# Exact products in three passes of 256 columns, or in one of 512 and one of 256

## The chip, the cores and the metric

One Trainium2 chip, one core. The metric is the device time of one execution of the whole program in microseconds (us); the median of the runs counts, and less is better.

## What is computed

A transformer of two different blocks on 256 tokens of width 1024, in fp32 throughout. Block 1 is an FFN (SwiGLU), a mixer (pooling and dilated attention, with gates) and a second FFN, each ahead of a residual sum with modulated norms. Block 2 is two layers of a mixer (retention, windowed attention, latent attention) and a mixture of 16 experts.

```python
def swiglu(u, w_in, w_out):
    a, b = jnp.split(u @ w_in, 2, axis=-1)
    return (jax.nn.silu(a) * b) @ w_out
...
        u = modulate(rmsnorm(h, g_norm_ffn1[l]), sh1, sc1)
        h = h + 0.5 * gt1 * swiglu(u, w_ffn1_in[l], w_ffn1_out[l])
        u = modulate(rmsnorm(h, g_norm_mix[l]), sh2, sc2)
        h = h + gt2 * token_mixing(u, cos, sin, w_in[l], w_pool[l], pool_scale[l],
                                   w_pool_branch[l], w_attn_branch[l], w_out[l])
```

The output is compared with an fp32 result, so that the large products have to keep nearly all the bits of fp32.

## The kernel before

**Layout.** Activations are held transposed: a tile of 128 features by 256 tokens is a block, and a tensor of width 1024 is eight blocks. Weights come from HBM in panels of 1 MB (1024 rows by 256 columns) into `raw` tiles, of which there are five (`raw_tile`, line 208).

**Exact products.** An fp32 number is split into a high part, rounded to the type fp32r, and the low rest (`split`, line 253): a cast on ScalarE and a subtraction on VectorE, both recorded at line 254. Weights are split half a panel at a time into `hl` tiles, of which there are six (`weights`, line 214); the raw tile is free when both halves are split. A product of a 128 by 128 block of weights with a block of activations is then three passes of TensorE into the same 256 columns of PSUM, low times low being left out:

```python
        def mm3(o, wh, wl, xh, xl, first, last):
            PE.matmul(o, wh, xh, start=first, stop=False)
            PE.matmul(o, wh, xl, start=False, stop=False)
            PE.matmul(o, wl, xh, start=False, stop=last)
```

These are lines 249 to 251. Where the tokens are the rows of the output, the activations are the stationary operand and the weights stream past: `proj_n` (lines 674 to 676) and `natural` (lines 1025 to 1027). Each pass loads its own stationary operand.

**PSUM** has eight banks of 512 fp32 columns. `mmtile` takes one of two banks in turn as two halves of 256 columns; the other six serve norms, attention and the like. Nothing reads a bank while passes into it are open, so the two halves of a bank are finished together.

**Stages.** The *first FFN* (`ffn`, line 552) begins with three pairs of panels as the modulation comes in (`begin`); from pair 3 on, a pair `a`, `b` of panels gives two feature blocks, one after the other, with `a` and `b` in the halves of one bank. ScalarE applies Silu to the first half (line 589), VectorE multiplies the second by it (line 590), and the product is split into the tiles gh and gl. Its output half runs over eight feature blocks: 22 block products into the first half of a bank, then one VectorE step that adds the gated sum to the residual hT (line 604), then the operand of the next step (`lead.add`) and its square for the norm. The *second FFN* does the same for pairs 1 to 10, after an opening pair.

The *first mixer* (`mixer`, line 704) computes queries and keys (two blocks of a panel in the halves of a bank, then `rotate`), values and the pool branch (`proj_n`, two token blocks in a bank), then for four heads the scores, the two gates (line 813, Tanh over the whole bank at line 815) and the values, then merges the branches and runs the output projection (line 837, VectorE step at line 838). In the FFNs and the mixer further columns of the modulation are computed on the side by VectorE from 1 MB tiles of w_ada (`ada`, line 354), some steps at a time where the code says `drain`; they use raw tiles too.

The *mixers of block 2* (`mixer2`, line 1014) use `natural` and `transposed` in the same way. Their output projection takes a panel at a time with its two feature blocks in one bank, the blocks of the inner dimension in the order 2, 3, 4, 5, 0, 1, 6, 7 (the attention outputs that are ready first come first), for panels 0 to 2, and one bank for each feature block in panel 3; VectorE adds the sums to hT (line 1319), and TensorE transposes finished blocks (line 1284) for the router. The *experts* (lines 1502 on) don't use these products.

**Order of the work.** The program is written in dataflow order; a planner puts each engine's instructions in a fixed order by its own estimate of when each becomes ready, earlier ones in the text first, and adds the semaphores. On the chip each engine works through its list and waits where an operand isn't ready. All weights are fetched from the queue of SyncE (SP).

Of the kernel before, what the change touches and what calls it, by code (L numbers as in the profile page):

```python
# [37 lines left out]
    # rotate-half permutation for two stacked heads of 64  # L38
# [9 lines left out]
    # partial sums: rows 0 and 32 of one kind, 64 and 96 of another  # L48
# [26 lines left out]
    # trailing mean minus token, transposed: [token in, token out]  # L75
# [9 lines left out]
    # retention decay with the 1/sqrt(dk) of the keys, [key, query]  # L85
# [9 lines left out]
    # router helpers: iota - 512 over slots; the lead by which f comes before e in a group of four  # L95
# [23 lines left out]
def layout(inputs):  # L119
    """Only moves data: every array keeps its type and values."""  # L120
# [27 lines left out]
    pair = [0, 3, 1, 4, 2, 5]      # heads whose keys lie in the first / second half, in turn  # L148
# [24 lines left out]
# ---------------------------------------------------------------- kernel  # L173
def body(tc, A, out, dbg=None, stop=None):
# [3 lines left out]
    with ctx:  # L178
# [22 lines left out]
        # ------------------------------------------------------------ streams  # L201
# [12 lines left out]
        class weights:  # L214
            """fp32 weights [128, kb, n] from DRAM, split exactly into hi + lo, in two halves, of which
            some are made at once and the others when first used."""

            def __init__(self, ap, kb, n, by="c", made=2):
# [6 lines left out]
                self.parts = [None, None]  # L225
# [4 lines left out]
            def make(self, i):  # L230
                if self.parts[i] is None:
# [5 lines left out]
                    self.parts[i] = (h, l)  # L237
                return self.parts[i]

            def at(self, k, a=None, b=None):  # L240
                """hi and lo of block k, columns a to b (all by default)."""
# [5 lines left out]
        def mm3(o, wh, wl, xh, xl, first, last):  # L247
            """o += w^T x, both operands split; only lo*lo (below fp32) is left to rounding."""
# [3 lines left out]

        def split(hi, lo, x):
            return S.copy(hi, x), V.tensor_tensor(out=lo, in0=x, in1=hi.bitcast(F32), op=ALU.subtract)  # L254

        def xtile(tag, dt=F32R, name=None):
            """[128, KB, T + 2], or that much of another use."""
            return xp.tile([P, KB * (T + 2)], dt, name=name or tag, tag=tag)

        class Lead:  # L260
            """A tensor's split product with its gains, made block by block as its sums become known: the first
            products of the next step run on it, and what is the same for all features of a token is applied to them.
            Further columns, an even number, hold vectors that are added to each token, so that their products come along.
            The normalised tensor takes its place."""

            def __init__(self, scale, extra=()):
                h, l = (xtile(t).rearrange("p (k t) -> p k t", k=KB) for t in ("xh", "xl"))
                self.h, self.l = h[:, :, :T], l[:, :, :T]
# [12 lines left out]
            def products(self, ws, banks, ks):  # L281
                """Of the four blocks of columns of two panels, a bank each."""
# [10 lines left out]
        # ------------------------------------------------------------ start  # L293
# [72 lines left out]
        def busy(n, tag="w"):  # L366
            """Keeps the clock of the tensor engine up over a wait: products that nothing reads."""
# [36 lines left out]
        class Norm:  # L404
            """Mean square over features of a transposed [128, KB, T] tensor, block by block."""
# [26 lines left out]
        def rows_to(rb, r):  # L432
            """Per-token columns [128, 2] as a row over all partitions: PSUM [128, T]."""
# [7 lines left out]
        def row(rb):  # L441
            """A row from PSUM in SBUF."""
# [4 lines left out]
        def lead_in(nrm, i, lead, ws, banks):  # L447
            """The first products, and the normalised tensor in place of their operand: rmsnorm(h) * scale + shift."""
# [9 lines left out]
        def norm_mod(rb, h, i, hi, lo):  # L458
            """hi + lo = rmsnorm(h) * scale + shift."""
# [7 lines left out]
        def first_rstd():  # L467
            """1 / rms of the input, as a row."""
# [83 lines left out]
        def ffn(f, nrm, i, side, n_in, n_out, lead, then, pq, start=None):  # L552
            with tc.tile_pool(name=f, bufs=1, reuse_waits="tile") as pool:
# [11 lines left out]
                for j in range(NJ):  # L565
# [1256 lines left out]
```

## Time and profile before

| | |
|---|---|
| time, median of 3 runs | 1182.7 us (1182.67 to 1187.75) |
| profiled execution, span (its own time is shown as the span alone) | 1186.2 us |
| TensorE (PE) busy | 1144.6 us, 96%, 8495 passes |
| weight loads (PEld) busy | 943.5 us, 80% |
| VectorE (DVE) busy | 713.3 us, 60% |
| ScalarE (ACT) busy | 511.4 us, 43% |
| GpSimd (POOL) busy | 44.5 us, 4% |
| mean granted TensorE clock | 0.987 of 2.4 GHz |
| HBM | 269.63 MB read, 228 GB/s over the span |

The profile is one execution, taken by the hardware profiler. A pass of TensorE is shown from its start to the modelled end of its result, and passes overlap: their mean length (some 280 ns) is not what each costs in a row of many; that is the distance from start to start, called pitch here. An engine's idle time is put down to the instruction that ended it.

### The profile page before, as it was taken

Reading aid. Unit: us, or ns where it says so; the run is one execution under the profiler, and the core shown is the slowest. Engines: PE = TensorE matmul, PEld = TensorE weight load, DVE = VectorE, ACT = ScalarE, POOL = GpSimd, SP = SyncE. Lnnn points to the kernel's source line nnn. Section 1 sums busy time; section 2 is a strip of 40 time slices with the busy share of each in tenths; the row PEclk is TensorE's granted clock in tenths of the full one; section 3 lists DMA queues with packets and bytes.
Section 4 is the critical chain, followed back from the end, with each engine's and each line's share of the span. In section 5 each row is a group of like instructions: output and inputs, shape, how many; then the busy total and the mean of one; then the engine's idle time right before and its main releaser. Section 6 shows DMA issues by size and latency. Waiting matters only on the chain. (4 is left out here: it accounts for less than half of the span.)

```text
span 1186.2 us, 20785 instructions
## 1 busy us (share of the span) xinstructions
PE 1144.6 (96%) x8495; PEld 943.5 (80%) x8495; DVE 713.3 (60%) x1410; ACT 511.4 (43%) x946; POOL 44.5 (4%) x53
## 2 busy tenths in 40 slices
PE   6999999999999999999999998999989999899995
PEld 4999999988888999999997878544458787844443
DVE  5698879777877775555677754621258864451114
ACT  4454445534534554444556434222247643322213
POOL 0000001000000200000120001000001000100000
PEclk9999999999999999999999999999989999999998
DMA  9788779738863455535572439599743334779941
GB/s 317 292 362 307 288 258 325 263 133 316 306 230 112 173 180 182 184 125 183 168 250 99 143 109 353 216 385 390 290 155 135 136 109 170 288 272 397 380 156 38
DMA packets 77354, 272.12 MB, mean 229 GB/s; under 512 B 7873, under 2 KB 10817, under 8 KB 62914
## 3 DMA queue, kind: packets, MB, share of 16 engines
q1 hardware_dynamic: 77250, 270.70, 62.8%
q8 instruction: 70, 1.15, 0.4%
q14 instruction: 34, 0.28, 0.1%
HBM read 269.63 MB, written 1.05 MB: 228 GB/s over the span
## 5 line engine op out<-in xcount | busy, mean ns | idle before, releaser
L254 DVE TENSOR_TENSOR hl<-raw,hl 128x1024 fp32r<-128x1024 f32 (+5 forms) x267 | 293.4, 1108 | 120.8 <-ACT hl L254 120.0
L254 ACT CAST hl<-raw 128x1024 fp32r<-128x1024 f32 (+5 forms) x267 | 254.0, 958 | 233.9 <-PE mm L251 172.2
L249 PE MATMUL mm<-xh,hl 128*128 128x256 f32 x896 | 255.2, 286 | 4.0 <-ACT xh L254 3.3
L251 PE MATMUL mm<-xh,hl 128*128 128x256 f32 x896 | 255.2, 285 | 0.0
L250 PE MATMUL mm<-xl,hl 128*128 128x256 f32 x896 | 253.4, 283 | 0.0
L249 PEld LDWEIGHTS mm<-xh,hl 128*128 128x128 f32 x896 | 169.6, 190 | 6.6 <-ACT xh L254 3.6
L250 PEld LDWEIGHTS mm<-xl,hl 128*128 128x128 f32 x896 | 170.4, 190 | 1.9 <-issue 1.9
L251 PEld LDWEIGHTS mm<-xh,hl 128*128 128x128 f32 x896 | 170.4, 190 | 1.0 <-issue 1.0
L1632 PE MATMUL gu<-hl,xg 128*64 128x512 f32 x208 | 101.8, 604 | 0.0
L249 PE MATMUL mm<-gh,hl 128*128 128x256 f32 x352 | 99.2, 282 | 0.0
L251 PE MATMUL mm<-gh,hl 128*128 128x256 f32 x352 | 99.2, 282 | 0.0
L250 PE MATMUL mm<-gl,hl 128*128 128x256 f32 x352 | 99.2, 282 | 0.0
L1632 PE MATMUL gu<-raw,xg 128*64 128x512 f32 x192 | 92.9, 603 | 0.0
L354 DVE SCALAR_TENSOR_TENSOR raw<-raw,cond 128x1024 f32<-128x1024 f32 x64 | 76.7, 1219 | 10.0 <-DMA raw<-in_w_ada_dram 10.0
L1668 DVE SCALAR_TENSOR_TENSOR ysl<-dn,gsl,ysh 128x512 fp32r<-128x512 f32 x32 | 23.9, 750 | 75.8 <-ACT ysh L1667 75.8
L250 PEld LDWEIGHTS mm<-gl,hl 128*128 128x128 f32 x352 | 67.0, 190 | 0.0
L249 PEld LDWEIGHTS mm<-gh,hl 128*128 128x128 f32 x352 | 67.0, 190 | 0.0
L251 PEld LDWEIGHTS mm<-gh,hl 128*128 128x128 f32 x352 | 67.0, 190 | 0.0
L1632 PE MATMUL gu<-rawe,xg 128*64 128x512 f32 x112 | 54.6, 604 | 0.0
L1619 DVE TENSOR_SCALAR xg<-ga,cols 128x256 f32<-128x256 f32 x32 | 17.4, 543 | 55.8 <-ACT xg L1618 55.8
L1667 ACT ACTIVATE ysh<-dn,gsl 128x512 fp32r<-128x512 f32 x32 | 22.0, 687 | 55.7 <-PE dn L1665 55.7
L1618 ACT ACTIVATE xg<-ga,cols 128x256 f32<-128x256 f32 x32 | 18.1, 565 | 60.9 <-PE ga L1615 55.0
(531 smaller groups left out, 2428.3 us busy)
## 6 DMA issues: line engine op xcount, KB each, us to landing
raw<-in_w_ffn_in_dram SPq DMA_DIRECT2D x41, 1024.0 KB, 4.9
raw<-in_w_ada_dram SPq DMA_DIRECT2D x34, 1024.0 KB, 6.2
raw<-in_w_in_dram SPq DMA_DIRECT2D x34, 1024.0 KB, 5.0
hl<-in_gate_up_dram SPq DMA_DIRECT2D x26, 1024.0 KB, 8.5
raw<-in_gate_up_dram SPq DMA_DIRECT2D x24, 1024.0 KB, 7.9
raw<-in_w_ffn_out_dram SPq DMA_DIRECT2D x32, 704.0 KB, 4.2
rawe<-in_gate_up_dram SPq DMA_DIRECT2D x14, 1024.0 KB, 8.2
raw<-in_w_out_dram SPq DMA_DIRECT2D x12, 1024.0 KB, 4.9
```

The lines of the kernel that those rows point to most:

```text
L249: PE.matmul(o, wh, xh, start=first, stop=False)
L250: PE.matmul(o, wh, xl, start=False, stop=False)
L251: PE.matmul(o, wl, xh, start=False, stop=last)
L254: return S.copy(hi, x), V.tensor_tensor(out=lo, in0=x, in1=hi.bitcast(F32), op=ALU.subtract)
L354: V.scalar_tensor_tensor(out=w, in0=w, scalar=1.0, in1=cond, op0=ALU.mult, op1=ALU.mult, accum_out=mod[:, a + j:a + j + 1])
L1618: S.activation(out=xg[:, 2 * j], in_=p[:, :T], func=AF.Identity, scale=col(0, 2 * j), bias=col(8, 2 * j))
L1619: mark[0] = V.tensor_scalar(out=xg[:, 2 * j + 1], in0=p[:, T:], scalar1=col(0, 2 * j + 1), scalar2=col(8, 2 * j + 1), op0=ALU.mult, op1=AL ...
L1632: mm = PE.matmul(p[i * CAP:(i + 1) * CAP], xg[:, k, s], w[i][:, k % 4], start=(k == 0), stop=(k == KB - 1))
L1667: made = S.activation(out=ysh[:, c], in_=p, func=AF.Copy, scale=gc)
L1668: mark[0] = made, V.scalar_tensor_tensor(out=ysl[:, c], in0=p, scalar=gc, in1=ysh[:, c].bitcast(F32), op0=ALU.mult, op1=ALU.subtract)
```

## The change

The three passes become two. The high and the low part of a tensor now lie in one tile, so that a block of both is one operand of 512 columns: the high weights meet both parts side by side in one pass that fills a whole bank, and the low weights then meet the high part in the second half of it (`mm3w`). The bank's halves are added when it is emptied, by a copy on ScalarE and an add on VectorE (`total`), or by two VectorE steps instead of one where the sum goes into hT. Where the weights stream, the high and low weights of a block lie side by side in the hl tile (`side_by_side`, `proj_v`).

Changed are the FFN input pairs that come after the opening ones, the FFN output halves, all projections of the first mixer but the opening queries and keys and the branch merge, `natural` and `transposed`, and panels 0 to 2 of the output projections of block 2. As a product of 256 columns now fills a bank, each takes a bank of its own; in the FFN input halves they rotate over six banks (first FFN) and four (second FFN). The tiles xh and xl become one tile x2, in turn with what reused them, gh and gl become gx, the first mixer's qT and kT (and mh and ml in their place) become one, and mixh and mixl become mix.

```diff
+                    self.both[i] = hl.rearrange("p (x m) -> p x m", x=2)[:, :, :w].rearrange("p x (k n) -> p x k n", n=c1 - c0)
...
+        def mm3w(o, wh, wl, x, first, last):
+            PE.matmul(o, wh, x, start=first, stop=False)
+            PE.matmul(o[:, 1], wl, x[:, 0], start=False, stop=last)
+
+        def total(out, o):
+            S.copy(out, o[:, 0])
+            return V.tensor_tensor(out=out, in0=out, in1=o[:, 1], op=ALU.add)
...
-        def xtile(tag, dt=F32R, name=None):
-            return xp.tile([P, KB * (T + 2)], dt, name=name or tag, tag=tag)
+        def xtile(dt=F32R, name="x2"):
+            return xp.tile([P, 2 * KB * (T + 2)], dt, name=name, tag="x2")
...
+                free = [("mm", ps)] * 2 + ([("b1", pq)] * 2 + [("b2", pq)] * 2 if start else [("b", pq)] * 2)
...
-                        pp = [mmtile() for s in range(2)]
-                        bk = [[(pp[s][:, 0], wa, s * P), (pp[s][:, 1], wb, s * P)] for s in range(2)]
                     for s in range(2):
                         if j not in done:
-                            proj_k(bk[s:s + 1], uh, ul)
+                            ab2 = [own(), own()]
+                            for o, w in zip(ab2, (wa, wb)):
+                                proj_w(o, w, s * P, lead_x)
...
+                        if pp is None:
+                            total(sa, ab2[0])
+                            S.activation(out=sa, in_=sa, func=AF.Silu)
+                            total(g, ab2[1])
+                            V.tensor_tensor(out=g, in0=g, in1=sa, op=ALU.mult)
...
-                            mm3(p[:, 0], *w.at(k), gh[:, b], gl[:, b], b == 0, b == FB - 1)
-                    V.scalar_tensor_tensor(out=hT[:, m], in0=p[:, 0], scalar=col(i + 2, m), in1=hT[:, m],
-                                           op0=ALU.mult, op1=ALU.add)
+                            mm3w(p, *w.at(k), gx[:, :, b], b == 0, b == FB - 1)
+                    for a in range(2):
+                        V.scalar_tensor_tensor(out=hT[:, m], in0=p[:, a], scalar=col(i + 2, m), in1=hT[:, m],
+                                               op0=ALU.mult, op1=ALU.add)
...
+        def proj_w(o, w, a, x, ks=range(KB)):
+            for k in ks:
+                mm3w(o, *w.at(k, a, a + P), x[:, :, k], k == ks[0], k == ks[-1])
+
+        def proj_v(w, xh, xl, t):
+            o, s = mmtile(), slice(t * P, (t + 1) * P)
+            for k in range(KB):
+                wx = w.side_by_side(k)
+                PE.matmul(o, xh[:, k, s], wx, start=(k == 0), stop=False)
+                PE.matmul(o[:, 1], xl[:, k, s], wx[:, 0], start=False, stop=(k == KB - 1))
+            return o
...
-                        p = mmtile()
-                        proj_t(p[:, 0], wgp, s * P, uh, ul)
-                        proj_t(p[:, 1], wga, s * P, uh, ul)
-                        S.activation(out=tg[:, 2 * i + s], in_=p, func=AF.Tanh, scale=0.5)
+                        for x, w in enumerate((wgp, wga)):
+                            p, o = mmtile(), tg[:, 2 * i + s, x * T:(x + 1) * T]
+                            proj_w(p, w, s * P, lead_x)
+                            total(o, p)
+                            S.activation(out=o, in_=o, func=AF.Tanh, scale=0.5)
...
-                    p = mmtile()
                     if i < 3:
-                        proj_k([[(p[:, s], w, s * P) for s in range(2)]], mixh, mixl, (2, 3, 4, 5, 0, 1, 6, 7))
+                        pw = [mmtile() for s in range(2)]
+                        for k in (2, 3, 4, 5, 0, 1, 6, 7):
+                            for s in range(2):
+                                mm3w(pw[s], *w.at(k, s * P, s * P + P), mix[:, :, k], k == 2, k == 7)
+                    else:
+                        p = mmtile()
...
-                        V.tensor_tensor(out=hT[:, m], in0=hT[:, m], in1=p[:, s], op=ALU.add)
+                        for o in ((p[:, s],) if i == 3 else (pw[s][:, 0], pw[s][:, 1])):
+                            V.tensor_tensor(out=hT[:, m], in0=hT[:, m], in1=o, op=ALU.add)
```

## Rows read from the trace of the kernel before

**Rows 1.** The page: span, and busy time by engine.

```profile
span 1186.2 us, 20785 instructions
PE 1144.6 (96%) x8495; PEld 943.5 (80%) x8495; DVE 713.3 (60%) x1410; ACT 511.4 (43%) x946; POOL 44.5 (4%) x53
```

**Rows 2.** Groups of instructions by line and form, TensorE: busy us, mean ns; idle before.

```profile
L249 PE MATMUL mm<-xh,hl 128*128 128x256 f32 x896 | 255.2, 286 | 4.0 <-ACT xh L254 3.3 <-DVE sa L584 0.7
...
L249 PE MATMUL mm<-gh,hl 128*128 128x256 f32 x352 | 99.2, 282 | 0.0
...
L249 PE MATMUL mm<-mixh,hl 128*128 128x256 f32 x128 | 37.2, 296 | 0.0
...
L1025 PE MATMUL mm<-hl,xh 128*128 128x256 f32 x96 | 27.3, 284 | 0.0
...
L249 PE MATMUL mm<-mh,hl 128*128 128x256 f32 x64 | 18.0, 284 | 0.7 <-DVE e L827 0.7
```

**Rows 3.** Timeline, second FFN: start us, us, engine, line.

```profile
440.16 0.28 PE L249 MATMUL mm<-xh,hl 128*128 128x256 f32 x1
...
445.89 0.28 PE L249 MATMUL mm<-xh,hl 128*128 128x256 f32 x1
```

**Rows 4.** Busy time by window: PE, PEld, DVE, ACT, POOL, granted clock, DMA share, GB/s.

```profile
66.00:158.00 92.00, 92.00 (x772) 92.00 (x771) 81.28 (x151) 43.70 (x71) 0.00 (x0) 1.00 0.80 302
158.00:221.00 63.00, 63.00 (x528) 63.00 (x527) 50.47 (x81) 31.74 (x51) 5.29 (x7) 1.00 0.84 296
295.00:367.00 72.00, 71.96 (x515) 61.43 (x515) 52.54 (x106) 32.38 (x55) 0.00 (x0) 1.00 0.65 245
380.00:403.00 23.00, 23.00 (x192) 23.00 (x193) 20.48 (x28) 13.66 (x24) 5.81 (x6) 1.00 0.62 211
417.00:595.00 178.00, 177.86 (x1492) 177.89 (x1493) 101.48 (x143) 87.93 (x136) 5.69 (x6) 1.00 0.50 173
```

**Rows 5.** Timeline of TensorE, first mixer of block 2: wider products.

```profile
631.88 0.29 PE L674 MATMUL ckv<-hl,xh 128*128 128x288 f32 x1
...
633.33 0.29 PE L676 MATMUL ckv<-hl,xh 128*128 128x288 f32 x1
...
651.33 0.34 PE L675 MATMUL ukv<-hl,cTl 128*128 128x384 f32 x1
...
652.03 0.34 PE L676 MATMUL ukv<-hl,cTh 128*128 128x384 f32 x1
```

**Rows 6.** Timeline of TensorE ahead of the router: bf16 filler products.

```profile
735.45 1.28 PE L370 MATMUL busy<-identb 128*128 128x128 bf16 x20
...
736.56 0.44 PE L435 MATMUL acc<-k_c_mats,nmu 128*128 128x128 f32 x2
```

**Rows 7.** Groups by line and form, ScalarE and VectorE, reads of a bank.

```profile
L590 DVE TENSOR_TENSOR g<-mm,sa 128x256 f32<-128x256 f32 x38 | 15.8, 417 | 2.4 <-ACT sa L589 2.4
...
L589 ACT ACTIVATE sa<-mm 128x256 f32<-128x256 f32 x38 | 14.3, 377 | 3.7 <-PE mm L251 3.6
...
L604 DVE SCALAR_TENSOR_TENSOR hT<-mm,mods,hT 128x256 f32<-128x256 f32 x16 | 7.7, 478 | 0.0
...
L1319 DVE TENSOR_TENSOR hT<-hT,mm 128x256 f32<-128x256 f32 x16 | 6.2, 417 | 22.9 <-PE mm L251 22.9
```

**Rows 8.** Timeline of VectorE, gates of the first mixer.

```profile
338.08 1.22 DVE L354 SCALAR_TENSOR_TENSOR raw<-raw,cond 128x1024 f32<-128x1024 f32 x1
...
342.79 1.22 DVE L254 TENSOR_TENSOR hl<-raw,hl 128x1024 fp32r<-128x1024 f32 x1
```

**Rows 9.** Timeline, output projection of block 2's first mixer.

```profile
701.99 0.36 PE L251 MATMUL mm<-mixh,hl 128*128 128x256 f32 x1
...
711.90 0.42 DVE L254 TENSOR_TENSOR mixl<-y,mixh 128x256 fp32r<-128x256 f32 x1 [1.36 <-ACT mixh L254]
...
713.42 0.75 DVE L1319 TENSOR_TENSOR hT<-hT,mm 128x256 f32<-128x256 f32 x2 [1.10 <-PE mm L251]
713.46 0.28 PE L250 MATMUL mm<-mixl,hl 128*128 128x256 f32 x1
```

More of the change, by code (lines that the diff above doesn't have):

```diff
@@ L224, in __init__ @@
                     self.cut = [(0, (kb + 1) // 2, 0, n), ((kb + 1) // 2, kb, 0, n)]
-                self.parts = [None, None]
+                self.parts, self.both = [None, None], [None, None]
                 self.last = ()
@@ L237, in make, with side_by_side @@
                     self.parts[i] = (h, l)
+                    self.both[i] = hl.rearrange("p (x m) -> p x m", x=2)[:, :, :w].rearrange("p x (k n) -> p x k n", n=c1 - c0)
                 return self.parts[i]
+            def side_by_side(self, k):
+                for i, (k0, k1, _, _) in enumerate(self.cut):
+                    if k0 <= k < k1:
+                        self.make(i)
+                        return self.both[i][:, :, k - k0]
             def at(self, k, a=None, b=None):
@@ L553, in ffn, with own @@
             with tc.tile_pool(name=f, bufs=1, reuse_waits="tile") as pool:
-                uh, ul = lead.h, lead.l
-                gh = pool.tile([P, FB, T], F32R, name="gh")
-                gl = pool.tile([P, FB, T], F32R, name="gl")
+                uh, ul, lead_x = lead.h, lead.l, lead.x
+                gx = pool.tile([P, 2, FB, T], F32R, name="gx")
+                gh, gl = gx[:, 0], gx[:, 1]
+                free = [("mm", ps)] * 2 + ([("b1", pq)] * 2 + [("b2", pq)] * 2 if start else [("b", pq)] * 2)
+                turn = [0]
+                def own():
+                    tag, of = free[turn[0] % len(free)]
+                    turn[0] += 1
+                    return bank(tag, "wide", of).rearrange("p (a t) -> p a t", a=2)
                 win, wout = A[f"w_{f}_in"], A[f"w_{f}_out"]
@@ L720, in mixer @@
                 psc = load("pool_scale", [P, 2], pool=pool)
-                qT, kT = (pool.tile([P, KB, T], F32, name=n, tag=n)[:, :6].rearrange("p (g s) t -> p g s t", g=3) for n in ("qT", "kT"))
+                qkT = pool.tile([P, 2, KB, T], F32, name="qkT", tag="qkT")
+                qT, kT = (qkT[:, i, :6].rearrange("p (g s) t -> p g s t", g=3) for i in range(2))
                 v = pool.tile([P, 3, 2, T], F32, name="v")
@@ L836, in mixer @@
                         p = mmtile()
-                        proj_t(p[:, 0], w, s * P, mh, ml)
-                        V.scalar_tensor_tensor(out=hT[:, m], in0=p[:, 0], scalar=col(5, m), in1=hT[:, m],
-                                               op0=ALU.mult, op1=ALU.add)
+                        proj_w(p, w, s * P, mx2)
+                        for a in range(2):
+                            V.scalar_tensor_tensor(out=hT[:, m], in0=p[:, a], scalar=col(5, m), in1=hT[:, m],
+                                                   op0=ALU.mult, op1=ALU.add)
                         lead.add(m)
@@ L1098, in mixer2 @@
                 p = natural(more[0])
-                evac(sv, p[:, :, :P])
-                evac(cq[:, :, :P], p[:, :, P:])
+                for t in range(2):
+                    total(sv[:, t], p[t][:, :, :P])
+                    total(cq[:, t, :P], p[t][:, :, P:])
                 pp = swa(0)
-                evac(cq[:, :, P:], natural(more[1]))
+                p = natural(more[1])
+                for t in range(2):
+                    total(cq[:, t, P:], p[t])
                 q_side = latent(cq, 384, 0, qn)
@@ L1187, in mixer2 @@
                 p = transposed(0)
[L1188 removed]
+                rotate(rqT, p, cos2, sin2, pool, pq, p)
                 pp = mla(0)
                 p = transposed(1)
[L1191 removed]
+                rotate(rkT, p, cos2, sin2, pool, pq, p)
                 mla_v(0, pp)
@@ L1194, in mixer2 @@
                 p = natural(weights(win[2], KB, 256, "k"))
-                evac(rv, p)
+                for t in range(2):
+                    total(rv[:, t], p[t])
                 p = transposed(3)
@@ L1478, in moe @@
                         lead = None if last else Lead(g(16), (cols[:, 16:24], cols[:, 24:32]))
-                    dst = xtile("xh", F32, "y").rearrange("p (k t) -> p k t", k=KB)[:, :, :T] if last else None
+                    dst = xtile(F32, "y")[:, :KB * (T + 2)].rearrange("p (k t) -> p k t", k=KB)[:, :, :T] if last else None
                     def finish():
```

61 lines of the change are left out of this document (27 added, 34 removed).

## The prediction, made before the change was run

> **What bounds the kernel now.** I read the page's busy times first: TensorE has work on it for 96% of the span, VectorE for 60%, ScalarE for 43% [rows 1]. The reader is to see that no other engine is near the span as a whole. A busy share of pipelined products can hide idle time, so I read the waits of TensorE next: the largest groups of the products that the change touches have 4.0 us of idle time ahead of 896 of them and none ahead of 352 [rows 2], nothing against 1186.2 us. Then the pitch: in the second FFN 48 products of 256 columns start between 440.16 and 445.89, 119.4 ns each, at granted clock 1.00, so at 2.4 GHz [rows 3, 4]. TensorE there is a conveyor; what shortens the conveyor shortens the kernel, as long as nothing else falls behind. So the last view is VectorE's share by stage [rows 4]: 81.28 of 92 us in the first FFN's input half, 20.48 of 23 in the first mixer's output projection, 52.54 of 72 in its gates, but 101.48 of 178 in the second FFN. The change gives TensorE less work and VectorE more, so these stages decide.
>
> **What is removed.** A block of an exact product is three passes of 256 columns now; it becomes one of 512 and one of 256. Blocks changed, by counts of the first passes [rows 2] and the code: of the 896 on xh the 32 of the opening pair of panels stay, so 864; 352 of the FFN output halves; 96 of 128 on mixh (the last panel of each layer stays); 96, 64 and 64 of the other three groups (the second of 64, at line 674, has a row like the one shown). Sum 1536: the FFN input halves 256 and 320, the output halves 352, the first mixer 320, the two later mixers 288.
>
> What one block saves hangs on the pitch of a 512-column pass, which no row shows for this type. Two widths stand beside 256: 288 columns (11 steps from 631.88 to 633.33, 131.8 ns) and 384 columns (4 steps from 651.33 to 652.03, 175 ns) [rows 5]. From 256 to 384 a column costs 55.6/128 = 0.434 ns, so 512 columns are 119.4 + 256 x 0.434 = 230.6 ns, and a block saves 238.8 - 230.6 = 8.2 ns: **12.6 us** over 1536 blocks. I take that, since 384 is the nearest width. The ends: if the added columns run at the pure 2.4 GHz, 226.1 ns, 12.7 saved, 19.5 us; if a pass costs in proportion to its columns, nothing. Slower than proportional is excluded by the 384 row, which is cheaper than 1.5 x 119.4 = 179 ns. The unit of weights is loaded twice instead of three times, but the 288- and 384-column passes have the same load as the 256-column ones and still differ in pitch, so the load isn't what paces them, and I give nothing for it.
>
> The pitch of small products shows how little a fixed part can be: 20 bf16 products of 128 columns start in the 1.11 us from 735.45 to 736.56 [rows 6], 55.5 ns each, 2.2 ns above 128 columns at 2.4 GHz. The Trainium skill ("TensorE: Matmul & The Clock Gate", section "Back-to-back issue gap") gives nearly that, columns at 2.4 GHz plus about 2.5 ns, for an isolated pass of any width. By that rule a block would save 2.5 ns and the kernel 3.8 us instead of 12.6. The trace doesn't agree for these passes: 119.4 ns, where the rule has 109.2.
>
> **What is added.** Every finished bank holds two halves. Where they are summed into SBUF this is one ScalarE copy (near 377 ns, the row of an activation that reads the same shape) and one VectorE add (417 ns) [rows 7]: 32 banks in the first FFN, 40 in the second, 32 in the first mixer, 28 in the later two, 55 us of VectorE in all. Where they go straight into the residual it is one more VectorE step, 478 ns 16 times in the FFNs and 8 times in the mixer, 417 ns 12 times in block 2 [rows 7]. ScalarE is at most six tenths busy in the stages of [rows 4] (13.66 of 23 us), and I cost its part at nothing but latency; if that cover goes, it is a copy's 0.38 us a bank.
>
> First FFN, input: VectorE needs 81.28 + 32 x 0.417 = 94.6 us, and TensorE now only 92 - 256 x 0.0082 = 89.9: 4.7 us too much. The output half has 63 - 1.5 - (50.47 + 8 x 0.478) = 7.2 us to spare, and the modulation columns (line 354) aren't needed by TensorE at once, so they can slide there; they hold raw weight tiles while they slide, which is why I don't call it free. Six banks rotate here, so the turn of a bank doesn't matter. I take 2 us, ends 0 and 4.7.
>
> First mixer, 32 banks in rotation of two. A bank fills in 8 x (230.6 + 119.4) ns = 2.8 us, and in that time the other must be copied and added, 0.8 us plus what stands ahead on VectorE's in-order queue. That queue shows long runs: from 338.08 to 344.0 five instructions of 1.22 us [rows 8]. With one ahead the bank is back in time, with two (2.44) it is 0.47 us late. Ends 0 and 32 x 0.47 = 15 us; I take a fifth, 3 us, since VectorE's share of this stage is 73% and not 100%. Its output projection needs 20.48 + 8 x 0.474 = 24.3 us (the step there is the FFN's with another gate) against 23 - 0.5: 1.8 us over. I take 1, since weight splits run ahead by up to six half tiles; ends 0 and 1.8.
>
> Second FFN: 101.48 + 40 x 0.417 + 8 x 0.478 = 122 of 174 us; nothing. At its end, and at the ends of the two stages ahead of it, the last feature block has one step of 0.48 us more before the norm can be closed; the opening products on blocks 0 to 6 cover it. I take 0.5 us, without cover it is 1.4.
>
> Later mixers: their output projection takes both banks of the pair for one panel, where now a panel has one and the next panel fills the other. Now TensorE goes on at 713.46 while the sums of the last panel begin at 713.42 [rows 9]. After the change the next panel waits for two dependent adds: 0.28 us of the product's own end + 2 x 0.417 - one pitch = 1.0 us, three times a layer. Transposes of finished blocks stand there to fill part of it, so I take 0.6 x 6 = 3.6 us, ends 0 and 6.
>
> No DMA is added or moved, and no order on SP's or POOL's queue; the merging of the two operand tiles into one changes which tile an allocation waits for, but both halves have the same last reader. Nothing for it.
>
> **Sum**: -12.6 + 2 + 3 + 1 + 0.5 + 3.6 = -2.5 us. The profiled execution's span is 1186.2 us, 3.5 us above the median of 1182.7 and inside the spread of the runs shown; I lay the difference on the median: **1180.2 us**. The bound for faster or slower, 0.5%, is 5.9 us: below 1176.8, above 1188.6.
>
> **Rivals.** (a) *Faster: the emptying hides everywhere.* The modulation columns take all of VectorE's delay and the banks come back in time. Then only the handovers and about 0.3 us a panel remain, 2.3 us: 1182.7 - 12.6 + 2.3 = 1172.4, or 1165.5 if a block saves 12.7 ns. For it: TensorE hardly waits now although VectorE has long runs ahead of short steps. Against it: those stages are already near 90% full.
>
> (b) *Slower: the turn of a bank on VectorE's queue.* In the first mixer every one of 32 banks is late by 0.47 us, since two long instructions stand ahead of each add: 15 us instead of 3, 1192.2. It decides from 2.0 us of work ahead of an add on. For: [rows 8]. Against: the order is planned with the adds known, and an engine at 73% [rows 4] has gaps.
>
> (c) *The wide pass saves nothing.* Passes cost in proportion, or keep only a fixed part of 2.2 ns [rows 6]: 12.6 or 9.2 us of the gain go, 1192.8 or 1189.4. Against: [rows 5]. The rule of the Trainium skill named above is near the second of these, with 1189.0.
>
> (d) *The change doesn't do what it says, since the operand is held as a whole.* A wide pass reads both parts in one strided view. If that view is ordered against all writes of its tile and not against those of its block, the output projection of the later mixers can't start early. Now its first products start before 702 us while the last block of its operand is written from 711.90 [rows 9]: up to 9.9 us a layer, half of it covered by the attention that runs then, +10: 1190. I have nothing for it but that possibility.
>
> **How the numbers follow.** Forecast (most of the saving given back) 0.44, (a) 0.36, (b) 0.09, (c) 0.06, (d) 0.05. (a) gives faster 0.36, the forecast the same 0.44, (b) to (d) slower 0.20. The forecast's own range is 1176 to 1187; the range for 8 in 10 reaches into (a) down to 1167 and up to (b) at 1192, and leaves out the ends of (a), (c) and (d). I give (a) much because four of the five losses are taken between ends of which one is nothing.
>
> **What would show it.** Right: about 1536 fewer products; a 512-column pitch near 231 ns; second FFN shorter by some 4 us with no new waits; waits of TensorE for VectorE's adds in the first mixer, and of about half a microsecond between panels in the later mixers. Wrong: a pitch near 239 or 226, VectorE idle in the first FFN's input, or waits of the output projection on mix tiles before 712.

## The result, and the profile after

The changed kernel takes 1194.6 us (median, 1191.4 to 1199.6) beside 1182.7 us for the kernel before on the same chip: a ratio of 1.0082, 95% interval 1.0055 to 1.011. It is slower by 0.8%, where 1180.2 us was forecast, and outside the range given (1167 to 1192). The profiled execution has a span of 1197.7 us.

The page of the changed kernel, span and busy time, answers to [rows 1]: TensorE has 1536 passes fewer, as counted, and is busy 3.9 us less; VectorE has 58 us more and ScalarE 37 us more.

```profile
span 1197.7 us, 17989 instructions
PE 1140.7 (95%) x6959; PEld 866.6 (72%) x6959; DVE 770.9 (64%) x1574; ACT 548.2 (46%) x1070; POOL 45.1 (4%) x53
```

Groups by line and form, TensorE, in the place of [rows 2]. The reader is to see the last column, idle time ahead: the products of the output projections (mix) now have idle time ahead of them that they did not have before, and so has the first mixer (x).

```profile
L263 PE MATMUL wide<-x,hl 128*128 128x512 f32 x576 | 204.0, 397 | 0.7 <-DVE sa L617 0.7
...
L263 PE MATMUL mm<-gx,hl 128*128 128x512 f32 x352 | 123.3, 395 | 0.0
...
L263 PE MATMUL mm<-x,hl 128*128 128x512 f32 x288 | 107.1, 411 | 1.2 <-DVE lt L269 1.2
...
L263 PE MATMUL mm<-mix,hl 128*128 128x512 f32 x96 | 37.0, 421 | 3.3 <-DVE mix L272 3.3
```

Busy time by window (columns as in [rows 4]), four stretches of nothing but changed products: input and output of the first FFN, then of the second. In each TensorE is busy throughout, so the length over the passes is the price: 110 us for 624 passes, 312 blocks, is 352.6 ns a block, where three passes of 119.4 ns [rows 3] are 358.2. By the same division the four stretches have 353.2, 351.2, 352.6 and 345.2 ns a block.

```profile
70.00:150.00 80.00, 80.00 (x453) 69.68 (x453) 77.35 (x154) 48.22 (x90) 0.00 (x0) 1.00 0.81 294
157.00:216.00 59.00, 59.00 (x336) 51.13 (x335) 53.08 (x94) 30.28 (x46) 7.66 (x7) 1.00 0.85 312
421.00:531.00 110.00, 110.00 (x624) 95.80 (x623) 80.50 (x127) 67.02 (x124) 0.00 (x0) 1.00 0.48 166
534.00:592.00 58.00, 58.00 (x336) 51.07 (x335) 37.61 (x54) 30.56 (x45) 4.49 (x6) 1.00 0.53 178
```

The added steps, by line and form, in the place of [rows 7], have the durations taken: 374 ns a copy, 418 ns an add, 480 and 418 ns the steps into the residual.

```profile
L638 DVE SCALAR_TENSOR_TENSOR hT<-mm,mods,hT 128x256 f32<-128x256 f32 x32 | 15.4, 480 | 0.3
...
L1373 DVE TENSOR_TENSOR hT<-hT,mm 128x256 f32<-128x256 f32 x28 | 10.3, 418 | 30.3 <-PE mm L264 20.4 <-PE mm L259 10.0
...
L269 DVE TENSOR_TENSOR lt<-lt,mm 128x256 f32<-128x256 f32 x20 | 8.4, 418 | 4.3 <-ACT lt L268 4.2
...
L268 ACT COPY lt<-mm 128x256 f32<-128x256 f32 x20 | 7.4, 374 | 33.5 <-PE mm L264 33.5
```

**Where the time came from.** I took the start of the first product of each stage in both traces and compared the lengths of the stages, against the terms of the forecast. The last column is the same kernel profiled once more (the first run below).

| stage (us against before) | forecast | after | again |
|---|---|---|---|
| first FFN, input from pair 3 on | -0.1 | -1.1 | -1.1 |
| first FFN, output | -1.4 | -1.2 | -1.2 |
| three handovers | +0.5 | +1.2 | +1.0 |
| first mixer, to the branch merge | +0.9 | +4.3 | +1.5 |
| merge and output projection | +0.5 | -0.3 | -0.1 |
| second FFN, input | -2.6 | -1.4 | -1.4 |
| second FFN, output | -1.4 | -1.6 | -1.6 |
| mixers of block 2, to the product rrb | -1.6 | -1.1 | -1.0 |
| from rrb to the router (product pos), two layers | +2.8 | +11.4 | +11.5 |

The table leaves out the opening (-0.7 us, and -3.5 in the second profile) and the experts (+1.9 and +1.1), which no edit touches; with them the stages add up, but for rounding, to the differences of the spans, 11.5 and 5.0 us.

One stage stands out. From rrb to pos the kernel before takes 40.5 us in each layer, the changed one 45.3 and 47.2. TensorE in the kernel before, layer 0: the start and the end of the stage, and the products on mix that run up to the transposes (tr) without a wait.

```profile
700.89 1.13 PE L1234 MATMUL rrb<-k_c_mats,r 128*128 128x128 f32 x8 [1.00 <-DVE r L1229]
...
708.95 0.28 PE L249 MATMUL mm<-mixh,hl 128*128 128x256 f32 x1
709.10 0.30 PE L1000 MATMUL tr<-k_c_mats,pr 128*128 128x128 f32 x1
...
741.40 0.17 PE L1406 MATMUL pos<-selb,ltb 128*128 128x16 bf16 x1 [3.01 <-DVE selb L1396]
```

The same stage in the changed kernel, layer 0:

```profile
699.11 1.13 PE L1283 MATMUL rrb<-k_c_mats,r 128*128 128x128 f32 x8 [0.51 <-DVE r L1278]
...
703.47 0.28 PE L264 MATMUL mm<-mix,hl 128*128 128x256 f32 x1
704.49 0.50 PE L263 MATMUL mm<-mix,hl 128*128 128x512 f32 x1 [0.75 <-DVE mix L272]
...
705.89 0.28 PE L264 MATMUL mm<-mix,hl 128*128 128x256 f32 x1
707.54 0.30 PE L1050 MATMUL tr<-k_c_mats,pr 128*128 128x128 f32 x1 [1.37 <-DVE pr L1028]
...
709.30 0.57 PE L1057 MATMUL y<-pt,vm 128*64 128x128 f32 x3
710.79 0.50 PE L263 MATMUL mm<-mix,hl 128*128 128x512 f32 x1 [0.92 <-DVE mix L272]
...
711.48 0.28 PE L264 MATMUL mm<-mix,hl 128*128 128x256 f32 x1
712.65 0.41 PE L1333 MATMUL xtr<-k_c_mats,hT 128*128 128x128 f32 x2 [0.89 <-PE mm L264]
...
744.38 0.17 PE L1460 MATMUL pos<-selb,ltb 128*128 128x16 bf16 x1 [3.01 <-DVE selb L1450]
```

The softmax of the last attention pair (tile pr) is a chain on VectorE and ScalarE that TensorE can't hasten: from rrb to its transposes (tr), the pair's score products included, it is 8.2 us before and 8.4 after. Before, TensorE fills it with products of panels 0 and 1 of the output projection, each in one bank. After, panel 0 has both banks. By the time the softmax is done the kernel before has issued 58 passes of this projection since its start, 19 blocks; the changed one 28, which are 14 blocks: the seven inner blocks that are ready, for two feature blocks. Nothing else could be opened, and TensorE stands still.

In layer 1 the granted clock then fell to half:

```profile
1012.20:1015.40 3.20, 3.20 (x12) 2.72 (x11) 1.85 (x2) 0.76 (x3) 0.00 (x0) 0.50 0.94 349
```

### The profile page after: what moved, and what is told of

Same layout as the page of the kernel before. It is cut to its first block, busy times and chain, and to the rows that moved or that the text cites. A ratio compares the mean times of both kernels' runs of the same rounds, so it can differ in the third digit from the quotient of the medians.

```text
span 1197.7 us, 17989 instructions
## 1 busy us (share of the span) xinstructions
PE 1140.7 (95%) x6959; PEld 866.6 (72%) x6959; DVE 770.9 (64%) x1574; ACT 548.2 (46%) x1070; POOL 45.1 (4%) x53
## 5 line engine op out<-in xcount | busy, mean ns | idle before, releaser
L263 PE MATMUL wide<-x,hl 128*128 128x512 f32 x576 | 204.0, 397 | 0.7 <-DVE sa L617 0.7
L264 PE MATMUL wide<-x,hl 128*128 128x256 f32 x576 | 162.4, 282 | 0.0
L263 PEld LDWEIGHTS wide<-x,hl 128*128 128x128 f32 x576 | 108.4, 188 | 26.9 <-ACT hl L272 0.9
L263 PE MATMUL mm<-gx,hl 128*128 128x512 f32 x352 | 123.3, 395 | 0.0
L264 PEld LDWEIGHTS wide<-x,hl 128*128 128x128 f32 x576 | 109.0, 189 | 0.2
L263 PE MATMUL mm<-x,hl 128*128 128x512 f32 x288 | 107.1, 411 | 1.2 <-DVE lt L269 1.2
L264 PE MATMUL mm<-gx,hl 128*128 128x256 f32 x352 | 98.6, 280 | 0.0
L264 PE MATMUL mm<-x,hl 128*128 128x256 f32 x288 | 82.5, 287 | 0.0
L263 PEld LDWEIGHTS mm<-gx,hl 128*128 128x128 f32 x352 | 66.1, 188 | 15.6
L263 PEld LDWEIGHTS mm<-x,hl 128*128 128x128 f32 x288 | 55.1, 192 | 15.9 <-issue 3.4
L264 PEld LDWEIGHTS mm<-gx,hl 128*128 128x128 f32 x352 | 66.3, 188 | 0.0
L704 PE MATMUL mm<-hl,x 128*128 128x512 f32 x160 | 57.5, 399 | 0.8 <-DVE cq L269 0.8
L264 PEld LDWEIGHTS mm<-x,hl 128*128 128x128 f32 x288 | 55.5, 193 | 1.6 <-issue 1.4
```

Source lines behind the costliest of these rows:

```text
L263: PE.matmul(o, wh, x, start=first, stop=False)
L264: PE.matmul(o[:, 1], wl, x[:, 0], start=False, stop=last)
L704: PE.matmul(o, xh[:, k, s], wx, start=(k == 0), stop=False)
```

## The experiments

**Theory after the result:** a product that takes a whole bank leaves half as many sums open, and where TensorE has to bridge a wait of another engine with ready products, it runs out of them. **Rivals:** the added steps on VectorE; the wide pass itself; something elsewhere that only shows here. All times stand against the kernel before on the same chip. The lengths are those from rrb to pos in layers 0 and 1; the blocks are those issued before the softmax's transposes in layer 0.

| run | ratio to before, 95% | rrb to pos, us | blocks |
|---|---|---|---|
| before | 1 | 40.5, 40.5 | 19.3 |
| changed kernel again | 1.0077 (1.0050 to 1.0103) | 45.3, 47.2 | 14 |
| three passes, a panel in one bank | 0.9951 (0.9935 to 0.9968) | 39.0, 39.4 | 23.3 |
| three passes, a panel in two banks | 1.0050 (1.0030 to 1.0070) | 44.1, 45.4 | 14 |
| two passes, panel 1 in other banks | 0.9987 (0.9970 to 1.0004) | 40.7, 41.4 | 17 |
| before, a panel in two banks | 1.0067 (1.0047 to 1.0087) | 43.9, 43.9 | 14 |

**The changed kernel again.** No edit.

> The changed kernel itself once more, beside the others on one chip. Expected: a ratio to the kernel before of 1.0055 to 1.011, as in the result. The profile is to show whether the clock drop at 240.7 to 247.6 comes in every execution: theory (it hangs on chance, since the run with own banks has the same code there and no drop): the stage from the first mixer's projections to its pool branch is 0.5 us or 3.2 us longer than before, by execution, and the drop at 1012 in the second output projection stays, because the idle gaps there are always there. Rival: both drops stay.

Measured: 1194.5 us, 1.0077. The drop of the clock in the first mixer was not there, the one in the output projection was, at 1005.7 to 1009.1; the first mixer's stages were +1.5 us and not +4.3. So the theory holds: 2.7 us of that stage come and go with the clock.

**Three passes in the output projections, a panel in one bank.**

```diff
-                        pw = [mmtile() for s in range(2)]
...
-                                mm3w(pw[s], *w.at(k, s * P, s * P + P), mix[:, :, k], k == 2, k == 7)
...
+                        proj_k([[(p[:, s], w, s * P) for s in range(2)]], mixh, mixl, (2, 3, 4, 5, 0, 1, 6, 7))
```

> Panels 0 to 2 of block 2's output projections back to three passes with a panel's two feature blocks in one bank; all else as in the changed kernel (1194.6 us). Theory (the loss of 4.75 and 6.7 us in the two output projections is made by that part): the part's 11.5 us go, its 96 blocks cost 0.8 us more in passes, so near 1184, and TensorE's granted clock stays at full speed in the second layer's output projection, where it was at half from 1012.2 to 1015.6. Rival (the loss comes from elsewhere, the operand tiles that became one or the order of the rest, and shows up only here): 1193 to 1195.

Measured: 1180.2 us, 0.9951, so by the ratios 0.0126 x 1185 = 15 us less than the changed kernel, and faster than the kernel before. The rest of the change pays. The gain is above the 10.7 us expected (11.5 less 0.8), since these stages are now shorter than before by 1.5 and 1.1 us: the parts ahead of them end sooner, and 23 blocks rather than 19 are issued in the softmax's time. Waits of TensorE from 692 to 734 us of this run:

```profile
PE pos L1456 <- DVE selb L1446: 3.0, 1, 3.0
PE rrb L1283 <- DVE r L1278: 0.5, 1, 0.5
```

**Three passes, but a bank for each feature block.** This takes away the wide pass and the second add, and leaves the banks.

```diff
-                                mm3w(pw[s], *w.at(k, s * P, s * P + P), mix[:, :, k], k == 2, k == 7)
+                                mm3(pw[s][:, 0], *w.at(k, s * P, s * P + P), mixh[:, k], mixl[:, k], k == 2, k == 7)
...
```

> Panels 0 to 2 of block 2's output projections in three passes again, with one add for a bank, but each feature block still in a bank of its own, so that a panel holds both banks. Theory (the bank is what is lost: no second panel can be open while the last attention outputs are made, and TensorE runs out of products): the loss stays nearly whole, 1194.6 + 0.8 for the passes - up to 2.4 for six adds fewer = 1193 to 1195.4, with idle gaps of about 1 us ahead of the mix products as before. Rival (it is the two dependent adds on VectorE's queue that TensorE waits for, or the wide pass itself): near the run with one bank a panel, 1184 to 1186.

Measured: 1191.0 us, 1.0050, with the waits of the changed kernel (691 to 737 us of this run):

```profile
PE tr L1050 <- DVE pr L1028: 1.6, 1, 1.6
PE s L1039 <- ACT qkm L733: 0.5, 1, 0.5
PE rrb L1283 <- DVE r L1278: 0.5, 1, 0.5
PE mm L258 <- DVE mix L272: 0.5, 1, 0.5
PE mm L257 <- ACT mix L272: 0.5, 1, 0.5
```

Most of the loss stays, and not "nearly whole": 1.2 us in layer 0 and 1.8 in layer 1, 3.0 us, go with the wide pass and its adds (in layer 1 the clock falls in both kernels, so there the figure is the less certain). Banks are the larger part; the rival holds a smaller one.

**Two passes, with panel 1 in the banks of the attention scores.**

```diff
-                        pw = [mmtile() for s in range(2)]
+                        if i == 1:
+                            s1 = pq.tile([P, 4, T], F32, name="s1", tag="s1", bufs=1)
+                            pw = [s1[:, 2 * s:2 * s + 2] for s in range(2)]
+                        else:
+                            pw = [mmtile() for s in range(2)]
```

> All as in the changed kernel, two passes everywhere; only panel 1 of block 2's output projections fills the two banks of the attention scores in place of the pair that all panels take in turn, so that a second panel can be open again. Theory (banks, not passes): most of the 11.5 us comes back, as with three passes in one bank, though these banks are free only when the last scores have been read: 8 to 12 us less than the changed kernel, ratio to the kernel before 0.996 to 1.001. Rival (two dependent adds, or the wide pass itself): within 3 us of the changed kernel, 1.004 to 1.010.

Measured: 1184.2 us, 0.9987, 0.0090 x 1186 = 10.7 us less than the changed kernel, which stood beside it. With every wide pass and every add kept, two more banks give most of it back. The waits of TensorE from 695 to 739 us of this run: those for the softmax are gone, one for a block of mix is left, and panel 1 waits 0.2 us for its banks.

```profile
PE mm L263 <- DVE mix L272: 0.7, 1, 0.7
PE s L1039 <- ACT qkm L733: 0.5, 1, 0.5
PE rrb L1283 <- DVE r L1278: 0.5, 1, 0.5
PE s L263 <- ACT pr L1019: 0.2, 1, 0.2
```

**The kernel before, with a bank for each feature block.** One resource taken away, nothing added.

```diff
-                    p = mmtile()
...
-                        proj_k([[(p[:, s], w, s * P) for s in range(2)]], mixh, mixl, (2, 3, 4, 5, 0, 1, 6, 7))
+                        pw = [mmtile() for s in range(2)]
+                        proj_k([[(pw[s][:, 0], w, s * P)] for s in range(2)], mixh, mixl, (2, 3, 4, 5, 0, 1, 6, 7))
...
```

> The kernel before with one edit: in panels 0 to 2 of block 2's output projections each feature block has a bank of its own, so that a panel holds both; three passes, no pass, add or copy more than before. Theory (banks alone): the two output projections get longer by the 5.1 and 6.0 us by which the run with own banks exceeded the run with one bank a panel, so 11 us slower than before, ratio 1.007 to 1.011. Rival (the loss needs the earlier stages of the changed kernel, which hand over sooner): under 1.004.

Measured: 1193.3 us, 1.0067: slower by 7.9 us, or 3.4 + 3.4 = 6.8 us by the two stages. The rival falls, and 14 blocks are early instead of 19. The theory's 11 was too much; it took in a drop of the clock in layer 1 of the run with own banks (from 994.7 us) and what the changed kernel's earlier stages gave the run with one bank a panel. The waits of its layer 0 (695 to 742 us):

```profile
PE tr L1000 <- DVE pr L978: 1.2, 1, 1.2
PE rrb L1234 <- DVE r L1229: 1.0, 1, 1.0
PE mm L249 <- ACT mixh L254: 0.5, 1, 0.5
PE mm L250 <- DVE mixl L254: 0.4, 1, 0.4
PE y L1006 <- ACT pt L685: 0.3, 1, 0.3
```

**The first mixer, queries and keys in three passes.** Right after its opening products TensorE stands still twice in the changed kernel (waits from 230.8 to 287 us), and in the profiled execution the clock is low there; the expectation has these two waits as 1.7 and 1.8 us:

```profile
PE perm L683 <- ACT lt L780: 1.4, 1, 1.4
PE mm L263 <- DVE lt L269: 1.2, 1, 1.2
```

```profile
240.00:247.00 7.00, 5.80 (x14) 3.90 (x14) 4.64 (x9) 0.00 (x0) 0.00 (x0) 0.55 0.34 112
```

```diff
-                            proj_w(p, w, s * P, lead_x)
-                            total(t[:, s], p)
...
+                        proj_k([[(p[:, s], w, s * P) for s in range(2)]], uh, ul)
```

> The first mixer's query and key projections (panels after the opening ones) back to three passes, two feature blocks in a bank; all else as in the changed kernel (1194.6 us). Theory (two idle stretches of 1.7 and 1.8 us ahead of the first rotation and the second product there bring TensorE's clock to half from 240.7 to 247.6, which is most of the 3.2 us that this stage lost): that clock drop and the 3.2 us go, 64 blocks cost 0.5 us more, near 1192. Rival (the idle time comes from the opening products and their rotation, which are the same in both): the drop stays, 1194.6 to 1195.2.

Measured: 1194.8 us, 1.0066 (1.0044 to 1.0088), which the interval doesn't tell from the changed kernel; the profile fell into other clock drops. The stage from the projections to the pool branch is 2.2 us shorter than before, where it was 0.4 (without a clock drop) or 3.2 us longer, and both idle stretches are gone: the rival's mechanism falls. The whole time is still the one that the rival gives; that the 2.6 us of the stage don't show in it stays open.

**The same products in two passes over four banks.**

```diff
+                        four = ("mm", "mm") if i == 0 else ("w", "st")
...
-                            p = mmtile()
+                            p = bank(four[s], "mm").rearrange("p (a t) -> p a t", a=2)
```

> All as in the changed kernel; only the queries and keys of the first mixer rotate over four banks (the pair and the two of the norms) in place of two. Theory (the same cause: two banks of one feature block each hold 5.6 us of products where they held 11.4, too little to cover the opening rotation): the two idle stretches of 1.4 and 1.2 us there go, with two passes kept, and the stage to the pool branch gets about 2.7 us shorter, a ratio 0.002 below that of the changed kernel. Rival (the idle time comes from two passes' adds on VectorE's queue): the stretches stay, same time as the changed kernel.

Measured: 1188.8 us, 1.0019 (1.0004 to 1.0033), and no wait of TensorE at all between 231 and 282 us. The stage is 2.9 us shorter than before, 3.3 less than in the changed kernel. The ratio fell by 0.0058, 6.9 us; the 3.6 us beyond the stage lie at the edge of what the two intervals allow, and I leave them open. Again the bank, not the pass.

**Both parts in three passes** (the edits of the second and the sixth run).

```diff
+                        proj_k([[(p[:, s], w, s * P) for s in range(2)]], mixh, mixl, (2, 3, 4, 5, 0, 1, 6, 7))
...
+                        proj_k([[(p[:, s], w, s * P) for s in range(2)]], uh, ul)
```

> Both parts back to three passes: block 2's output projections with one bank a panel, and the first mixer's queries and keys. Theory (the two losses are separate): 11.5 + 3.2 us go, 1.3 us of passes come back, near 1181, a little below the kernel before (1182.7). Rival (what one stage gives is taken back later, by weights that arrive no sooner or by a clock drop that moves): 1184 or more, no better than the run with the output projections alone.

Measured: 1176.5 us, 0.9927 (0.9903 to 0.9950). The rival's 1184 falls. By the ratios it is 2.8 us better than with the output projections alone, where 2.7 was expected; the two intervals overlap, so that the gains add is likely and not shown.

**Both parts in two passes, with the further banks.**

```diff
+                            pw = [s1[:, 2 * s:2 * s + 2] for s in range(2)]
...
+                            p = bank(four[s], "mm").rearrange("p (a t) -> p a t", a=2)
```

> Two passes everywhere, with the further banks of both other runs (panel 1 of block 2's output projections, the first mixer's queries and keys). Theory: both gains add and the 160 blocks keep their saving of 1.3 us, so as fast as the run with both parts in three passes, ratio to the kernel before 0.990 to 0.995. Rival (three passes in one bank are needed, since the added steps on VectorE cost there too): 0.998 or more.

Measured: 1181.9 us, 0.9960 (0.9946 to 0.9974): just above the range. The output projections take 40.7 and 41.4 us, 1.7 and 2.0 us more than with three passes in one bank. Only 17 blocks are early there, against 23, since the scores' banks come free late; how much of the difference is the rival's added steps, no run here separates.

**Each place in its better form:** three passes in the output projections, four banks in the first mixer.

```diff
+                        proj_k([[(p[:, s], w, s * P) for s in range(2)]], mixh, mixl, (2, 3, 4, 5, 0, 1, 6, 7))
...
+                            p = bank(four[s], "mm").rearrange("p (a t) -> p a t", a=2)
```

> Two passes but in block 2's output projections (three, one bank a panel), and the first mixer's queries and keys in two passes over four banks. Theory (each place gets the form in which most products are ready): 0.7 us better in the first mixer than with three passes there, as the stage from its projections to its pool branch read -2.85 against -2.16 us: ratio to the kernel before 0.990 to 0.994. Rival (the bank of the norms, held longer, delays something else): 0.995 or more.

Measured: 1175.4 us, **0.9922 (0.9902 to 0.9942)**, faster than both kernels; by the ratios 18 us less than the changed kernel. The interval doesn't tell it from the run with three passes in both parts: the 0.7 us stand only in the stage. Its page: 96 passes more than the changed kernel, and in these two executions 25 us less span (3.5 of it from the opening, which no edit touches).

```profile
span 1172.4 us, 18171 instructions
PE 1132.2 (97%) x7055; PEld 867.3 (74%) x7055; DVE 766.1 (65%) x1562; ACT 548.9 (47%) x1070; POOL 44.3 (4%) x53
```

**The gates in three passes too.**

```diff
-                            proj_w(p, w, s * P, lead_x)
-                            total(o, p)
...
+                        proj_t(p[:, 0], wgp, s * P, uh, ul)
+                        proj_t(p[:, 1], wga, s * P, uh, ul)
```

> As the run with four banks and three-pass output projections, and the first mixer's gates in three passes too, a bank for both gates of a block. Theory (the gates lose by two passes, since two banks in turn hold little there as well: the stage from the pool branch to the merge read +1.1 to +1.5 us though its 128 blocks should save 1.0): that stage gets back to 0 or less, 1 to 2 us better than the run without this. Rival (the copies and adds are hidden, and the stage's loss comes from the scores or the softmax ahead of them): the stage stays at +1 or gets longer by the passes.

Measured: 0.9936 (0.9916 to 0.9956), and the stage from the pool branch to the merge at +2.4 us instead of +1.2. My theory for the gates falls: by the stage they gain 1.2 us by two passes, which the two ratios can't tell. Why that stage is longer than before at all stays open; it begins where its neighbour ends, and some work has changed sides.

**Two passes in the FFNs alone** (the three mixers as before).

```diff
-                            proj_w(p, w, s * P, lead_x)
+                        proj_k([[(p[:, s], w, s * P) for s in range(2)]], uh, ul)
...
-                    return [proj_v(w, xh, xl, t) for t in range(2)]
```

> Only the two FFNs in two passes; all three mixers as in the kernel before. Theory (the wide pass pays wherever enough banks rotate; the FFNs have six and four, and give most of the saving): stages of the FFNs 5 to 6 us shorter, nothing lost later, ratio 0.994 to 0.997, so a little behind the run with four banks and three-pass output projections (0.990 to 0.994), which has the mixers' saving too. Rival (the saving is lost at later waits, on transfers above all): 0.998 or more.

Measured: 1182.1 us, 0.9971 (0.9956 to 0.9987). The FFN stages are -1.1, -1.2, -1.4 and -1.6 us, 5.3 in all, and every mixer stage is within 0.3 us of the kernel before. No later stage takes the saving back; the ratio shows 3.4 us of it (1.5 to 5.2).

## Why the prediction was wrong

- **The step that failed is the term "Later mixers", 3.6 us with ends 0 and 6**, and it failed at its upper end. It measured +11.5 with the passes' saving of 0.8 in it, so 12.3: 8.7 us too little, of the 14.4 between the forecast of -2.5 and the +11.9 measured. I had seen that a panel would take both banks, and priced the moment when a full bank waits for its adds, three times a layer. Such a wait is there, once a layer: 0.89 and 0.94 us ahead of xtr after panel 0, under 0.1 after the others. The wide pass and its adds together cost 3.0 us by the run with own banks, so near the 3.6 in size, though not at the three places. What I did not price is what the second bank was for: in the 8.2 us up to the last softmax's transposes it holds panel 1. That costs 3.4 us a layer (the kernel before with two banks a panel). The rest is the clock: the same code took 45.3 us in layer 0 with the clock full and 46.9 in the run where it fell there, and in layer 1 45.7 without a drop and 47.2 with one, so 1.5 us. Sum: 6.8 + 3.0 + 1.5 = 11.3 of the 11.5; the last two terms overlap a little, since the clock falls in layer 1 of the run with own banks too.
- [Rows 9] had it: products on mix tiles run before 702 us, ahead of tiles finished at 711.90. I read it for rival (d), whether they could still start early, and they do, at 683.86 us. The question to ask was how many of them can be open. One of the prediction's signs of being wrong is in the trace: the output projection waits for mix tiles ahead of 704.49 and 710.79, before 712. It stood there for (d); here it is a TensorE that has no other sum to go on with.
- **A block's saving** was 8.2 ns at a pitch of 230.6. From start to start the FFN inputs have medians of 233 to 234 and 118 ns, so the pitch was nearly right, and a few ns make the term. The four FFN stages gained 5.3 us where 928 blocks should have given 7.6: 5.7 ns a block, by stage from 4.3 (the second input) to 9.3 (the second output). At that price 1536 blocks give 8.8 us instead of 12.6, an estimate. Why the second FFN's output is cheaper than the other three stretches (345.2 ns a block beside 351.2 to 353.2), no run here shows. Rival (c) falls: two passes do pay. The Trainium skill ("TensorE: Matmul & The Clock Gate", section "Back-to-back issue gap") has 215.8 ns for a 512-column pass on its own, and the trace disagrees for this type, with medians of 229 to 235 ns.
- **First FFN input**, 2 us of delay (0 to 4.7): near nothing, as rival (a) has it. The stage gained 1.1 us of its 2.1, but the second FFN's input, for which no delay was forecast, gained 1.4 of 2.6, the same per block, and the 576 wide products of both have 0.7 us of idle time ahead of them. **First mixer**, 3 us: 1.5 + 2.1 = 3.6 at full clock, the right size for the wrong reason, so luck. No bank turned late in the rotation of the queries and keys (with four banks there is no wait, and with two the only waits are the two at the start; nor does TensorE wait from 287 to 362 us, in the gates); 2.6 us are the same open-sums effect while the opening rotation waits. Rival (b)'s mechanism therefore was not at work; its 0.47 us should also have read 0.43, 2.44 + 0.79 - 2.8, so 14 us instead of 15.
- **Handovers**, 0.5 us: 1.0 to 1.2, of which 0.7 to 1.0 is the second FFN's start, which is 0.0 in the run with two passes in the FFNs alone; near the uncovered end of 1.4. **Output projection of the first mixer**, 1 us (0 to 1.8): 0.2 to 0.4 by the forecast's saving of 0.5.
- **The chances.** The slower side had 0.20, given to (b) to (d), none of which happened. The rival that did was missing: too few open sums under a wait. It would have read: 8.2 us up to the softmax's transposes, two banks instead of four half banks, 14 of the 28 early blocks left, 5.3 blocks less than now at 358 ns, 1.9 us a layer at least (3.4 was measured).

The Trainium skill ("Perfetto Trace Analysis", section "Matmuls") advises to rotate matmul groups through banks so that emptying overlaps; the runs agree and add that banks also set how far TensorE can run ahead of a wait.

## What to carry to other kernels

A PSUM bank is not only a place to empty in time: the number of sums that can be open is TensorE's stock of ready work for the waits of other engines (here 14 blocks instead of 19, and 3.4 us a layer, with no instruction added). Before widening a product, list the waits that it bridges, count the ready blocks with the banks before and after, and give wide products to the stages with spare banks (the FFNs, 5.3 us) and keep narrow ones where a softmax or a rotation must be covered. A change that loses as a whole can be a gain in most of its parts: here 0.8% slower became 0.8% faster by reverting 96 blocks and giving 64 two banks more.

## What the runs showed of the hardware

- TensorE's clock fell to half after a cluster of idle gaps of 0.7 to 1.4 us (four of them from 1002 to 1011.6 in the changed kernel, with products between), and not each time: of the same code, layer 1 lost it in the two profiles of the changed kernel and in the run with queries and keys in three passes, layer 0 in the run with four banks, shown here, so four passages of eight. No profile of a kernel without those gaps has the drop between rrb and the wait of 3.0 us ahead of pos.

```profile
707.70:711.10 3.40, 3.40 (x12) 2.90 (x11) 2.03 (x2) 0.93 (x3) 0.00 (x0) 0.50 1.01 331
```

The Trainium skill ("TensorE: Matmul & The Clock Gate", section "A second HAM failure mode: psum-queue depth-cycling") tells of small idle stretches between groups of products that bring the clock down; the trace agrees, at 1.5 us a time.

- The opening of the program varies too: some of the profiles, that of the kernel before among them, have 7 to 10 us at half clock from about 28 us on, others none, and the stretch up to the first FFN's pair 3 ran from 4.7 us shorter to 1.9 us longer than in the kernel before, without an edit to it. Stage lengths, and not whole spans, are what two single profiles can be compared by.
